# First weight chunk of the output tails stored 64 bytes into its tile, and the first product of each seven-product half 264 columns wide in place of two operand copies

## The chip, the cores and the metric

The kernel runs on one core of a Trainium2 chip. The metric is the device time of one execution in microseconds (us), the median of several runs. The kernel before took 1624.95 us, the median of three runs between 1624.73 and 1625.51.

## What is computed

A two-layer diffusion transformer on 256 image tokens and 256 context tokens of width 1024. Each layer is a half feed-forward, a mixer (attention in layer 0, an mLSTM in layer 1) and another half feed-forward, each behind a modulation by two conditioning vectors and followed by a layer norm. The part that matters here is the feed-forward, cut from the reference:

```python
def half_ffn(h, shift, scale, gate, w_in, w_out, g, b):
    xm = modulate(h, shift, scale)
    a, u = jnp.split(xm @ w_in, 2, axis=-1)
    y = (jax.nn.silu(a) * u) @ w_out
    return post_norm(h, 0.5 * gate * y, g, b)
```

Its hidden width is 2816, that is 22 blocks of 128. It runs four times: twice in layer 0 and once in layer 1 for both token groups (512 columns), and once more, at the very end, for the image tokens alone.

## The kernel before

**Operands.** Everything is float32 in storage. A product that must be exact to float32 is made of three products in `float32r`: each operand is split into a high and a low part, and `mm3` (L239) issues high times high, high times low and low times high into one PSUM tile. Activations lie transposed, 128 rows of features by tokens, so a product has a stationary weight block of 128 by 128 and a moving operand of 256 columns (one token group, `LAT` or `CTX`) or 512 (`BOTH`). The activations' two parts stand in `xh` and `xl` (L281), each feature block 512 columns and 64 more.

**Weights.** A chunk is 128 rows by 1024 columns, eight stationary blocks. SP loads it into a `raw` tile; `chunk` (L218) takes a tile of the ring `w` of seven (L215; 2112 columns of 4 bytes, which is 66 times 128 bytes), ACT casts the chunk into its first half as the high part (L225), and DVE subtracts to leave the low part in the second half (L230). An argument `sh` moves both parts `sh` columns into the tile; `SH` is 16 columns, 64 bytes. `Stream` (L143) fetches chunks in order and keeps the last; `Keep` (L158) keeps all of them, for weights that two passes use.

**A feed-forward** (`ffn`, L684) works in two halves of eleven hidden blocks. For each half it makes the eleven blocks of the hidden layer (the `in` part) and then the eight output blocks `d` (the `out` part), each the sum of 11 blocks, so 33 products of `mm3`. The output weights of a half are eleven chunks of eight blocks, numbered `d * 11 + i`: chunk 5 holds numbers 40 to 47. In the second half the first four output blocks are made for 512 columns at once with a `Stream` that moves nothing (`sh` 0). The last four (`TAIL`, L56) are made twice, for the image tokens and then for the context tokens, with 256 columns each, so that the norm of the image tokens starts while the context tokens are still in work. I call these the image tail and the context tail. Their weights come through a `Keep` with `SH` (L782) that takes over the chunk which the `Stream` holds at that moment, chunk 5: numbers 40 to 43 belong to the last block of the body, 44 to 47 to the tail, twelve products in each of the two tails. So chunk 5 stands at the start of its tile, and the six chunks behind it 64 bytes further. Between the products of the tails stand the statistics products of the norm (L447), issued at fixed places of a table (`TAILSTEP`, L99), some with 256 moving columns and some with one.

**The seven-product form.** In the second feed-forward of layer 0 and the first of layer 1, the second half makes its hidden blocks by `fast_in` (L626): seven block products of a Strassen kind instead of eight, each over four feature blocks, so 7 x 4 x 3 = 84 products of 256 columns for a hidden block and 924 for a half. The products are a11, a12, s1, s2, a22, s4 and s3, in that order, twelve instructions each. The sums of activations that they need are made before by `fast_sums` (L599) into the operand `made` during the out part of the first half. All weights here have `SH`. For the first hidden block of the half alone (`j == NFH`, L631), a22 does not read its operand from `made[2]`: two ACT copies (L635) put it into a tile of the ring `w`, `FLIP` = 56 columns in, which is 32 bytes past a step of 64 bytes.

**What sets the order.** TensorE takes its products in program order. ACT and DVE follow an order that a scheduler makes from priorities and dependencies; the ring of seven `w` tiles sets how far ahead weights are split.

Of the kernel before, what the change touches and what calls it, by code (L numbers as in the profile page):

```python
# [9 lines left out]
F32 = mybir.dt.float32  # L10
F32R = mybir.dt.float32r
# [7 lines left out]
P = 128  # L19
D = 1024  # L20
ND = D // P
T = 512
TL = 256
LAT = (0, 256)
# [3 lines left out]
NFH = 11  # L28
# [3 lines left out]
BLOCK = 64  # L32

SH = 16
# [9 lines left out]
WB = 7  # L44
# [11 lines left out]
TAIL = 4  # L56
# [31 lines left out]

SUMSAT = 4
FLIP = 56  # L90
BESIDE = {1: (), 2: (2, 3)}
PIECES = 4
DOTS = {
# [79 lines left out]
class Body:  # L173
# [23 lines left out]
    def mm(self):  # L197
        return self.t([P, 512], tag="mm", bufs=6, pool=self.pp)
# [37 lines left out]
            edge = mybir.DependencyInfo(mybir.DependencyClass.NoSync, mybir.DependencyReason.DATA)  # L236
            self.tc.add_manual_dep(ins.ins, last.ins.name, edge, reason="behind the start")

    def mm3(self, out, w, x, first, last, pin=False, group=True):  # L239
        (wh, wl), (xh, xl) = w, x  # L240
        mm = lambda *k, **kw: self.nc.tensor.matmul(*k, skip_group_check=not group, **kw)  # L241
        ins = mm(out, wh, xh, start=first, stop=False)
        if pin:
            self.pin(ins)
        mm(out, wh, xl, start=False, stop=False)
        mm(out, wl, xh, start=False, stop=last)

    def x(self, d, g):
        return self.xh[:, d, g[0] : g[1]], self.xl[:, d, g[0] : g[1]]
# [342 lines left out]
    def fast_operands(self, st):  # L592

        n = ND // 2 * TL
        x = self.t([P, 6 * n], F32R, pool=st)
        self.t([P, FLIP], pool=st)
        self.made = [[x[:, (2 * i + p) * n : (2 * i + p + 1) * n].rearrange("p (k f) -> p k f", f=TL) for p in range(2)] for i in range(3)]
# [28 lines left out]
    def fast_in(self, j, w_in, st):  # L626

        nc, V, S = self.nc, self.nc.vector, self.nc.scalar
        half = 4 * P
        t4 = self.made[2]  # L630
        if j == NFH:  # L631
            w = self.t([P, 2 * 1024 + BLOCK], F32R, tag="w", bufs=WB)
            t4 = [w[:, FLIP + i * 1024 : FLIP + (i + 1) * 1024].rearrange("p (k f) -> p k f", f=TL) for i in range(2)]
            for i in range(2):
                S.copy(t4[i], self.made[2][i].bitcast(F32))  # L635
        r0, r1 = (self.raw(w_in[2 * j + i]) for i in range(2))
        sums = self.t([P, 4 * half], tag="sums", bufs=1, pool=st)
        part = lambda x, i: x[:, i * half : (i + 1) * half]
        a11, a21, a12, a22 = part(r0, 0), part(r0, 1), part(r1, 0), part(r1, 1)
        s1, s2, s4, s3 = (part(sums, i) for i in range(4))  # L640
        add = lambda o, x, y: V.tensor_tensor(out=o, in0=x, in1=y, op=ALU.add)  # L641
        ws = [self.pair(sh=SH, n=half)] + [self.pair(sh=SH) for _ in range(3)]
        self.split(a11, *ws[0])
        self.split(r1, *ws[1])
        add(s1, a21, a22)
        add(s2, s1, a11)
        add(s4, s2, a12)
        add(s3, a11, a21)
        self.split(sums[:, : 2 * half], *ws[2])
        self.split(sums[:, 2 * half :], *ws[3])  # L650
        w = {n: [part(x, i) for x in ws[p]] for n, p, i in (
            ("a11", 0, 0), ("a12", 1, 0), ("a22", 1, 1), ("s1", 2, 0), ("s2", 2, 1), ("s4", 3, 0), ("s3", 3, 1),
        )}
        of = lambda k0, g: lambda k: self.x(k0 + k, g)
        made = lambda i: lambda k: [x[:, k, :] for x in self.made[i]]

        def product(o, name, x, first, last):
            for k in range(ND // 2):
                c = slice(k * P, (k + 1) * P)
                self.mm3(o, [y[:, c] for y in w[name]], x(k), first and k == 0, last and k == ND // 2 - 1, group=False)  # L660

        x, yv, z = self.mm()[:, :TL], self.mm(), self.mm()[:, :TL]
        y, v = yv[:, :TL], yv[:, TL:]
        a, u = self.tmp(), self.tmp()
        product(x, "a11", of(0, LAT), True, False)
        S.copy(a[:, :TL], x)
        product(y, "a12", of(ND // 2, LAT), True, True)
        product(v, "s1", of(0, CTX), True, False)
        S.copy(u[:, TL:], v)
        product(x, "s2", made(0), False, False)  # L670
        S.copy(a[:, TL:], x)
        product(z, "a22", lambda k: [x[:, k, :] for x in t4], True, True)
        S.copy(u[:, :TL], z)
        product(v, "s4", of(ND // 2, CTX), False, True)
        V.tensor_tensor(out=a, in0=a, in1=yv, op=ALU.add)
        S.activation(a, a, AF.Silu)
        product(x, "s3", made(1), False, True)
        u2 = u.rearrange("p (n f) -> p n f", n=2)
        V.scalar_tensor_tensor(u2, x[:, None, :].broadcast_to([P, 2, TL]), -1.0, u2, ALU.mult, ALU.subtract)
        V.tensor_tensor(out=a, in0=a, in1=u, op=ALU.mult)  # L680
        gh, gl = self.gt[j] = tuple(self.t([P, self.gw], F32R, tag=k, bufs=self.gn, pool=self.gp) for k in ("gh", "gl"))
        self.split(a, gh, gl)

    def ffn(self, layer, s, gate, groups, side, start=None, cpool=None):  # L684
# [4 lines left out]
        with self.tc.tile_pool(name=f"ffn{li}", bufs=1) as gp:  # L689
# [32 lines left out]
            w_in, w_out = self.a["ffn_in"][li], self.a["ffn_out"][li]  # L722
            stream = lambda j: Stream(self, [w_in[2 * j + i] for i in range(2)])
            for hf in range(2):
                js = list(range(hf * NFH, (hf + 1) * NFH))[0 if hf else done :]
                if hf == 0 and not start:
                    first = js[:LEAD]
# [6 lines left out]
                    j = first[-1]  # L734
                    ps = unit_in(j, ws[j], LAT, ks=k0)
                    assert not self.running
                    xs = {}
                    for k in BESIDE[li]:
                        xs[k] = [self.t([P, self.gw], F32R, tag=t, bufs=self.gn, pool=gp)[:, FLIP : FLIP + TL] for t in ("gh", "gl")]
                        for o, x in zip(xs[k], self.x(k, CTX)):  # L740
# [20 lines left out]
                    self.residual(2, self.pin)  # L761
                if not hf:
                    self.residual(len(self.later))
                w = Stream(self, [w_out[hf * NFH + i] for i in range(NFH)])
                body = ND - TAIL if hf else ND
                if fast:
                    more.close()
# [13 lines left out]
                if body < ND:  # L781
                    w = Keep(self, w.chunks, SH, w)  # L782
# [1000 lines left out]
```

## Time and profile before

| | us |
|---|---|
| median of 3 runs | 1624.95 |
| profiled execution, its own time | 1624.66 |
| its span in the trace | 1622.9 |
| TensorE matmul busy | 1608.2 |
| TensorE weight loads busy | 1450.3 |
| VectorE busy | 1349.3 |
| ScalarE busy | 749.0 |
| the four copies of L635, ScalarE | 1.05 each |

The profiled execution is 0.29 us below the median, and 1.76 us of it lie outside the span. A matmul's record goes on after the next one has begun (0.276 to 0.39 us long, with a next start every 0.113 to 0.227 us), so the busy share of TensorE says little, and the pace of its products is what to read: where a view in order of time joins n equal products into one piece, the pace is the piece's length less one record's length, divided by n - 1. The view in order of time gives, in each row, the start in us from the span's start, the length in us, the engine, the line, the operation with its tiles and shapes, and the count.

### The profile page before, as it was taken

What the parts mean: (1) busy time and instruction counts of PE and PEld (TensorE: products, weight loads), DVE (VectorE), ACT (ScalarE), POOL (GpSimd) and SP (SyncE); (2) the same over time, 40 slices, a digit from 0 to 9 for tenths busy, and PEclk for the clock granted to TensorE, in tenths of its full rate; (3) what the DMA queues carried; (4) which work ended last, traced back from release to release, by engine and by line L of the source; (5) the groups of instructions that cost most, each with busy time, mean ns of one, the idle gap of its engine ahead of it and who ended that gap; (6) DMA issues with size and microseconds to landing.
All of it is one profiled execution on the core that took longest, in us unless ns stands there. A gap on an engine that the chain in (4) does not pass through costs nothing. (4 is left out here: it accounts for less than half of the span.)

```text
span 1622.9 us, 26548 instructions
## 1 busy us (share of the span) xinstructions
PE 1608.2 (99%) x10280; PEld 1450.3 (89%) x10280; DVE 1349.3 (83%) x2687; ACT 749.0 (46%) x1276; POOL 62.4 (4%) x77
## 2 busy tenths in 40 slices
PE   9999999999999999999999999999999999999998
PEld 7888888889988998889999998889999989999986
DVE  7899978648879879999976979689967968897597
ACT  6522132314676443316652443336642657566542
POOL 0000000001011200000000100000001000020000
PEclk9999999999999999999999999999999999999999
DMA  9677765422203347633354258723372343437562
GB/s 358 220 250 238 237 207 184 141 66 85 66 2 99 136 144 228 212 104 118 117 175 151 79 180 289 245 64 106 109 238 83 98 130 92 151 98 259 170 181 91
DMA packets 72222, 251.56 MB, mean 155 GB/s; under 512 B 7960, under 2 KB 10776, under 8 KB 72096
## 3 DMA queue, kind: packets, MB, share of 16 engines
q1 hardware_dynamic: 71520, 249.09, 48.0%
q8 instruction: 80, 1.31, 0.3%
q10 hardware_dynamic: 576, 0.79, 0.1%
q14 instruction: 46, 0.38, 0.1%
HBM read 248.79 MB, written 1.05 MB: 154 GB/s over the span
## 5 line engine op out<-in xcount | busy, mean ns | idle before, releaser
L241 PE MATMUL t<-t,t 128*128 128x256 f32 (+2 forms) x8340 | 1307.7, 318 | 3.2 <-ACT t L225 1.1
L241 PEld LDWEIGHTS t<-t,t 128*128 128x128 f32 x8340 | 1175.8, 188 | 120.7 <-ACT t L225 2.0
L225 ACT CAST t<-t 128x1024 fp32r<-128x1024 f32 (+3 forms) x509 | 421.6, 850 | 479.3 <-PE t L241 225.0
L230 DVE TENSOR_TENSOR t<-t,t 128x256 fp32r<-128x256 f32 (+2 forms) x728 | 505.4, 729 | 110.7 <-ACT t L225 106.9
L350 DVE SCALAR_TENSOR_TENSOR t<-t,t 128x1024 bf16<-128x1024 f32 x224 | 260.7, 1220 | 0.0
L588 ACT ACTIVATE t<-t 128x512 f32<-128x512 f32 (+1 forms) x71 | 34.4, 489 | 98.8 <-PE t L241 97.8
L941 PE MATMUL t<-t,t 128*128 128x256 f32 (+1 forms) x256 | 79.3, 310 | 0.2 <-ACT t L541 0.2
L718 DVE SCALAR_TENSOR_TENSOR t<-t,t,t 128x256 f32<-128x256 f32 x96 | 42.7, 478 | 43.9 <-PE t L241 43.7
L943 PE MATMUL t<-t,t 128*128 128x256 f32 (+1 forms) x256 | 78.5, 307 | 0.1
L942 PE MATMUL t<-t,t 128*128 128x256 f32 (+1 forms) x256 | 78.3, 306 | 0.1
L589 DVE TENSOR_TENSOR t<-t,t 128x512 f32<-128x512 f32 (+1 forms) x71 | 39.0, 553 | 40.6 <-PE t L241 27.7
L484 POOL TENSOR_TENSOR t<-t,t 128x256 f32<-128x256 f32 x30 | 23.2, 774 | 1105.1 <-ACT t L474 1103.8
L869 PE MATMUL t<-t,t 128*128 128x512 f32 (+1 forms) x300 | 61.0, 364 | 0.4 <-DVE t L863 0.4
L869 PEld LDWEIGHTS t<-t,t 128*128 128x128 f32 x300 | 51.3, 189 | 10.0 <-DVE t L863 1.1
L474 ACT ACTIVATE t<-t 128x256 f32<-128x256 f32 x72 | 26.1, 412 | 65.8 <-DVE t L467 65.8
L1470 PE MATMUL t<-t,t 128*128 128x512 f32 (+2 forms) x276 | 55.7, 357 | 0.0
L1470 PEld LDWEIGHTS t<-t,t 128*128 128x128 f32 (+1 forms) x276 | 44.9, 183 | 11.0 <-issue 1.1
L942 PEld LDWEIGHTS t<-t,t 128*128 128x128 f32 x256 | 48.1, 188 | 3.3 <-DVE t L230 0.8
L941 PEld LDWEIGHTS t<-t,t 128*128 128x128 f32 x256 | 48.2, 188 | 3.2 <-ACT t L541 0.4
L943 PEld LDWEIGHTS t<-t,t 128*128 128x128 f32 x256 | 48.1, 188 | 2.8 <-DVE t L542 0.3
L541 ACT ACTIVATE t<-t,t 128x256 fp32r<-128x256 f32 x72 | 32.8, 502 | 31.1 <-DVE t L540 31.1
L641 DVE TENSOR_TENSOR t<-t,t 128x512 f32<-128x512 f32 x66 | 45.3, 687 | 0.4
(211 smaller groups left out, 1107.8 us busy)
## 6 DMA issues: line engine op xcount, KB each, us to landing
t<-in_ffn_in SPq DMA_DIRECT2D x168, 512.0 KB, 4.1
t<-in_ada_w SPq DMA_DIRECT2D x138, 512.0 KB, 4.4
t<-in_ffn_out SPq DMA_DIRECT2D x66, 512.0 KB, 4.4
t<-in_ffn_last SPq DMA_DIRECT2D x22, 512.0 KB, 3.5
t<-in_att_in SPq DMA_DIRECT2D x12, 512.0 KB, 3.5
t<-in_att_out SPq DMA_DIRECT2D x8, 512.0 KB, 3.6
t<-in_ml_qk SPq DMA_DIRECT2D x8, 512.0 KB, 3.7
t<-in_ml_v SPq DMA_DIRECT2D x8, 512.0 KB, 3.6
```

The source lines that it names most:

```text
L225: self.behind(self.nc.scalar.copy(h, x))
L230: self.behind(self.nc.vector.tensor_tensor(out=ls, in0=xs, in1=hs.bitcast(F32), op=ALU.subtract))
L241: mm = lambda *k, **kw: self.nc.tensor.matmul(*k, skip_group_check=not group, **kw)
L350: ins = nc.vector.scalar_tensor_tensor(self.tmp().bitcast(BF16), r, 1.0, self.cb[:, v, :], ALU.mult, ALU.mult, accum_out=to)
L589: V.tensor_tensor(out=sl, in0=sl, in1=pu[:, :n], op=ALU.mult)
L641: add = lambda o, x, y: V.tensor_tensor(out=o, in0=x, in1=y, op=ALU.add)
L718: V.scalar_tensor_tensor(z, y[:, gg[0] - t0 : gg[1] - t0], gate()[:, v, d : d + 1], z, ALU.mult, ALU.add)
L869: pin(nc.tensor.matmul(o, gs[g], ws[k][w][:, i : i + n], start=k == k0 and g == w == 0, stop=k == k1 - 1 and g == 1,))
L941: mm(o, self.xh[:, k, c], wh, start=k == 0, stop=False)
L942: mm(o, self.xh[:, k, c], wl, start=False, stop=False)
L943: mm(o, self.xl[:, k, c], wh, start=False, stop=k == ND - 1)
L1470: mm = lambda *k, **kw: pin(nc.tensor.matmul(*k, **kw))
```

## The change

Two things are changed. First, the stream of output weights of a feed-forward moves one chunk by `SH`, in the second half only: the one whose number is (8 - 4) * 11 // 8 = 5. This holds for the three feed-forwards that `ffn` makes. Second, in `fast_in` the two copies and their tile are gone, and a22 reads `made[2]` for every hidden block. The first product of a11 of the first hidden block (high part times high part of feature block 0) gets 264 columns instead of 256: it reads eight columns more of `xh`, and writes eight more of its PSUM tile. No instruction reads those eight.

```diff
+ODD = 8
...
-    def mm3(self, out, w, x, first, last, pin=False, group=True):
+    def mm3(self, out, w, x, first, last, pin=False, group=True, wide=()):
...
-        ins = mm(out, wh, xh, start=first, stop=False)
+        o, y = wide or (out, xh)
+        ins = mm(o, wh, y, start=first, stop=False)
...
-        t4 = self.made[2]
-        if j == NFH:
-            w = self.t([P, 2 * 1024 + BLOCK], F32R, tag="w", bufs=WB)
-            t4 = [w[:, FLIP + i * 1024 : FLIP + (i + 1) * 1024].rearrange("p (k f) -> p k f", f=TL) for i in range(2)]
-            for i in range(2):
-                S.copy(t4[i], self.made[2][i].bitcast(F32))
...
-        x, yv, z = self.mm()[:, :TL], self.mm(), self.mm()[:, :TL]
+        xx, yv, z = self.mm(), self.mm(), self.mm()[:, :TL]
+        x = xx[:, :TL]
...
-        product(x, "a11", of(0, LAT), True, False)
+        product(x, "a11", of(0, LAT), True, False, (xx[:, : TL + ODD], self.xh[:, 0, : TL + ODD]) if j == NFH else ())
...
-        product(z, "a22", lambda k: [x[:, k, :] for x in t4], True, True)
+        product(z, "a22", made(2), True, True)
...
-                w = Stream(self, [w_out[hf * NFH + i] for i in range(NFH)])
+                w = Stream(self, [w_out[hf * NFH + i] for i in range(NFH)], lambda c, hf=hf: SH if hf and c == (ND - TAIL) * NFH // ND else 0)
```

In the order of instructions a row names the tile that is written, then those that are read (the moving operand, then the weights). On TensorE, at the hand-over from the first half's output blocks to the first hidden block of the seven-product half in layer 0, the order before is this (t_67 and t_68 are `xh` and `xl`, t_7095 the weights of a11, t_7111 its PSUM tile):

```order
L241 MATMUL t_7046<-t_6623,t_7058 128x512
L241 MATMUL t_7046<-t_6624,t_7058 128x512
L241 MATMUL t_7046<-t_6623,t_7058 128x512
L241 MATMUL t_7111<-t_67,t_7095 128x256
L241 MATMUL t_7111<-t_68,t_7095 128x256
L241 MATMUL t_7111<-t_67,t_7095 128x256 x2
```

And now (t_7092 are the weights of a11, t_7108 its PSUM tile):

```order
L242 MATMUL t_7046<-t_6623,t_7058 128x512
L242 MATMUL t_7046<-t_6624,t_7058 128x512
L242 MATMUL t_7046<-t_6623,t_7058 128x512
L242 MATMUL t_7108<-t_67,t_7092 128x264
L242 MATMUL t_7108<-t_68,t_7092 128x256
L242 MATMUL t_7108<-t_67,t_7092 128x256 x2
```

Only the width of one product differs; every other instruction of TensorE stands where it stood, in this half and everywhere else. The shift of chunk 5 changes addresses alone and no row.

On ACT, ahead of the same half, the order before is this (t_6876 is `made`, t_67 the context columns of `xh`, t_7087 the tile of the two copies, t_7095 to t_7098 the weights of the first hidden block):

```order
L225 CAST t_67<-t_6985 128x2x256
L225 CAST t_6876<-t_6987 128x512
L225 CAST t_6876<-t_6985 128x512
L225 CAST t_6876<-t_7000 128x512
L635 CAST t_7087<-t_6876 128x1024
L225 CAST t_7095<-t_7090 128x512
L635 CAST t_7087<-t_6876 128x1024
L225 CAST t_7096<-t_7092 128x1024
L225 CAST t_7097<-t_7094 128x1024
L225 CAST t_7098<-t_7094 128x1024
```

And now (t_7092 to t_7095 are the weights of the first hidden block):

```order
L226 CAST t_7092<-t_7087 128x512
L226 CAST t_7093<-t_7089 128x1024
L226 CAST t_67<-t_6919 128x2x256
L226 CAST t_6876<-t_6921 128x512
L226 CAST t_6876<-t_6919 128x512
L226 CAST t_6876<-t_6934 128x512
L226 CAST t_67<-t_6985 128x2x256
L226 CAST t_6876<-t_6987 128x512
L226 CAST t_6876<-t_6985 128x512
L226 CAST t_6876<-t_7000 128x512
L226 CAST t_7094<-t_7091 128x1024
L226 CAST t_7095<-t_7091 128x1024
```

The two copies are gone, and the casts of the first two weight tiles stand ahead of those of the activation sums instead of behind them; the matching subtractions on DVE move the same way.

More of the change, by code (lines that the diff above doesn't have):

```diff
@@ L655, in fast_in, with product @@
         made = lambda i: lambda k: [x[:, k, :] for x in self.made[i]]
-        def product(o, name, x, first, last):
+        def product(o, name, x, first, last, wide=()):
             for k in range(ND // 2):
                 c = slice(k * P, (k + 1) * P)
-                self.mm3(o, [y[:, c] for y in w[name]], x(k), first and k == 0, last and k == ND // 2 - 1, group=False)
-        x, yv, z = self.mm()[:, :TL], self.mm(), self.mm()[:, :TL]
+                self.mm3(o, [y[:, c] for y in w[name]], x(k), first and k == 0, last and k == ND // 2 - 1, group=False, wide=() if k else wide)
+        xx, yv, z = self.mm(), self.mm(), self.mm()[:, :TL]
+        x = xx[:, :TL]
         y, v = yv[:, :TL], yv[:, TL:]
         a, u = self.tmp(), self.tmp()
-        product(x, "a11", of(0, LAT), True, False)
+        product(x, "a11", of(0, LAT), True, False, (xx[:, : TL + ODD], self.xh[:, 0, : TL + ODD]) if j == NFH else ())
         S.copy(a[:, :TL], x)
```

## The prediction

> **What bounds the kernel now.** I first read the page's busy times and slices, then the groups by line and shape, then the order of time on TensorE around the two places that change.
>
> ```profile
> span 1622.9 us, 26548 instructions
> PE 1608.2 (99%) x10280; PEld 1450.3 (89%) x10280; DVE 1349.3 (83%) x2687; ACT 749.0 (46%) x1276; POOL 62.4 (4%) x77
> PEclk9999999999999999999999999999999999999999
> ...
> L241 PE MATMUL t<-t,t 128*128 128x512 f32 x2892 | 662.3, 390 | 0.0
> L241 PE MATMUL t<-t,t 128*128 128x256 f32 x5304 | 629.8, 279 | 2.9 <-ACT t L225 1.1 <-DVE t L542 1.0 <-ACT t L541 0.5
> ```
>
> TensorE always has a product in work, at the full granted clock, and the 5304 products of 256 columns from `mm3` waited 2.9 us in all. Wherever this holds, only two things can change the time: the number of products and the pace at which one follows the other. So I read the pace, a piece's length less one record, over the gaps in it. The rows are start, length, engine, line, operation and count. These are the first seven-product half's start, its middle and the piece between, then the same three of the second half; ahead of them the 512-column products that come before.
>
> ```profile
> 725.64 11.72 PE L241 MATMUL t<-t,t 128*128 128x512 f32 x51
> 738.34 7.34 PE L241 MATMUL t<-t,t 128*128 128x256 f32 x61
> 743.64 1.57 PE L241 MATMUL t<-t,t 128*128 128x256 f32 x12
> 746.32 96.95 PE L241 MATMUL t<-t,t 128*128 128x256 f32 x854
> 1090.43 5.35 PE L241 MATMUL t<-t,t 128*128 128x256 f32 x44
> 1095.73 1.34 PE L241 MATMUL t<-t,t 128*128 128x256 f32 x10
> 1097.95 97.29 PE L241 MATMUL t<-t,t 128*128 128x256 f32 x857
> ```
>
> 512 columns: (11.72 - 0.39) / 50 = 0.2266 us. The half begins at (7.34 - 0.28) / 60 = 0.1177 us a product and from 746.3 goes on at (96.95 - 0.28) / 853 = 0.1133 us to its end. The second half does the same: 0.1178 at first, then 0.1133. The two stretches have equal shapes, the same placing of weights and, in these rows, the same clock:
>
> ```profile
> core 0: us, PE busy (x) PEld busy (x) DVE busy (x) ACT busy (x) POOL busy (x), PEclk, DMA share, GB/s
> 738.60:745.50 6.90, 6.90 (x61) 6.90 (x60) 5.25 (x9) 4.01 (x7) 0.00 (x0) 1.00 0.37 113
> 746.50:843.00 96.50, 96.50 (x854) 96.50 (x854) 90.35 (x119) 61.85 (x101) 0.00 (x0) 1.00 0.38 121
> ```
>
> So a row of such products has two lasting paces, which I call the 118 pace and the 113 pace. What stands between them in both halves is the piece of twelve at 743.64 (and at 1095.73), the a22 product that reads the copies of L635, 32 bytes off a 64-byte step. It runs at (1.57 - 0.28) / 11 = 0.117 itself, and four products behind it the 113 pace is there.
>
> The tails show a third pace. Rows: the twelve products of chunk 5 in the image tails of the first two feed-forwards, each followed by the same tail's other products, and those twelve in the third.
>
> ```profile
> 348.34 1.12 PE L241 MATMUL t<-t,t 128*128 128x256 f32 x8
> 349.42 11.71 PE L241 MATMUL t<-t,t 128*128 128x256 f32 x98
> 873.29 1.24 PE L241 MATMUL t<-t,t 128*128 128x256 f32 x9
> 874.37 11.71 PE L241 MATMUL t<-t,t 128*128 128x256 f32 x98
> 1225.26 1.24 PE L241 MATMUL t<-t,t 128*128 128x256 f32 x9
> ```
>
> With weights at the start of their tile the pace is (1.12 - 0.28) / 7 = 0.120 and twice (1.24 - 0.28) / 8 = 0.120; with weights 64 bytes further it is (11.71 - 0.28) / 97 = 0.1178, the 118 pace. In the context tails, of the first feed-forward (two rows), the second (four) and the third (two):
>
> ```profile
> 362.00 2.17 PE L241 MATMUL t<-t,t 128*128 128x256 f32 x17
> 364.24 1.36 PE L241 MATMUL t<-t,t 128*128 128x256 f32 x10
> 887.17 1.98 PE L241 MATMUL t<-t,t 128*128 128x256 f32 x16
> 889.22 1.24 PE L241 MATMUL t<-t,t 128*128 128x256 f32 x9
> 890.54 0.87 PE L241 MATMUL t<-t,t 128*128 128x256 f32 x6
> 898.87 11.31 PE L241 MATMUL t<-t,t 128*128 128x256 f32 x93
> 1239.02 1.98 PE L241 MATMUL t<-t,t 128*128 128x256 f32 x16
> 1241.06 1.36 PE L241 MATMUL t<-t,t 128*128 128x256 f32 x10
> ```
>
> Ahead of chunk 5 the first is at the 118 pace, (2.17 - 0.28) / 16 = 0.118; the second and third are at the 113 pace, (1.98 - 0.28) / 15 = 0.1135. Chunk 5's twelve run at 0.120 (364.24, 889.22, 1241.06), and what follows them (890.54) is at (0.87 - 0.28) / 5 = 0.118: the twelve products have thrown the row out of the 113 pace.
>
> **The seven-product halves: the copies.** Two copies a half are removed, on ACT:
>
> ```profile
> L635 ACT CAST t<-t x4: 1047/1049/1056, 730.5 to 1081.7; 128x1024 fp32r<-128x1024 f32 x4
> ...
> who waited for it (us, times):
> ```
>
> That is 4 x 1.05 = 4.2 us of ACT, for which nobody waited; the first starts at 730.5, 7.8 us ahead of the row at 738.34, the last 8.7 ahead of that at 1090.43. I cost their removal at nothing. What hides them is the last 512-column products before the half (51 in the row of 725.64), and ACT is 46% busy. The ring of `w` tiles is used once less a half, so ACT and DVE split the first weights earlier and the activation sums later. Those sums are first needed by s2, 36 products or 4.2 us into the half, so I put no wait there.
>
> What the copies did for TensorE is the question. Without them a22 reads operands on a 64-byte step and, by the rows above, would leave the 118 pace alone. The wide first product must do their work.
>
> **The wide product itself.** Eight columns of 256 at the 113 pace are 8 x 0.1133 / 256 = 0.0035 us, 0.007 for both halves; as a whole further step of sixteen columns at most twice that.
>
> **What the wide product does to the pace.** No product in the trace is 264 columns wide, and none stands alone between 512 and 256 columns. The nearest rows are in the mLSTM's projections, where groups with products of 258 columns (L1340 and L1342, two columns past a step of 64 bytes) are followed directly by `mm3` products of 256 columns and 64-byte-shifted weights. There are seven such hand-overs; these are the rows of 256 behind each:
>
> ```profile
> 1356.20 2.20 PE L241 MATMUL t<-t,t 128*128 128x256 f32 x18
> 1361.78 2.20 PE L241 MATMUL t<-t,t 128*128 128x256 f32 x18
> 1369.40 2.40 PE L241 MATMUL t<-t,t 128*128 128x256 f32 x19
> 1375.33 2.32 PE L241 MATMUL t<-t,t 128*128 128x256 f32 x19
> 1383.22 2.20 PE L241 MATMUL t<-t,t 128*128 128x256 f32 x18
> 1388.85 4.70 PE L241 MATMUL t<-t,t 128*128 128x256 f32 x40
> 1397.27 3.56 PE L241 MATMUL t<-t,t 128*128 128x256 f32 x30
> ```
>
> Six give (2.20 - 0.28) / 17 = 0.113 or the like; the third gives (2.40 - 0.28) / 18 = 0.118. The copies were two of two. So a step of columns that is not whole sixteens ends in the 113 pace eight times in nine, and 512 columns followed straight by 256 at the 118 pace (738.34, 1090.43). I take it that the wide product brings the 113 pace, some five products behind it, and that it then lasts, as it does for 97 us. Gain a half: 64 products now at the 118 pace (48 ahead of a22, its twelve, four behind) less five, 59 x (0.1177 - 0.1133) = 0.26, less 0.004; both halves **-0.51 us**. The bounds: -0.28 a half at best; at worst the 118 pace for the 860 products behind the present change of pace, 860 x 0.0044 = +3.8 a half.
>
> The Trainium skill bears on this ("TensorE: Matmul & The Clock Gate", "Back-to-back issue gap"): it gives the warm gap of an isolated product by its columns alone, N / 2.4 + 2.5 ns, 109.2 for 256. By that the change would be the eight columns, 3.3 ns a half, and nothing else. The trace disagrees: 113.3, 117.7 and 120 ns for the same N at the same clock.
>
> **Chunk 5.** Twelve products in each of six tails go from 0.120 to the pace around them. In the image tail 512-column products come straight ahead, which in both halves above gave the 118 pace; then 12 x (0.120 - 0.1178) = 0.026 us, three times. The same in the first context tail. In the other two the 113 pace stands ahead and, without the twelve, should go on through them and the nine behind, up to the single-column statistics products: 12 x (0.120 - 0.1135) + 9 x (0.118 - 0.1135) = 0.078 + 0.041 = 0.12 us each. There it ends, by a like place in attention's tail: 0.114 ahead of those products ((0.96 - 0.28) / 6), 0.118 behind ((0.99 - 0.28) / 6).
>
> ```profile
> 541.65 0.96 PE L241 MATMUL t<-t,t 128*128 128x256 f32 x7
> ...
> 543.13 0.99 PE L241 MATMUL t<-t,t 128*128 128x256 f32 x7
> 374.44 7.42 PE L241 MATMUL t<-t,t 128*128 128x256 f32 x64
> ```
>
> Sum: 4 x 0.026 + 2 x 0.12 = **-0.34 us**. The twelve 512-column products of chunk 5 in each body (36 in all) get shifted weights, which no 512-column product of `mm3` has now. A weight load takes 0.19 us and their gap is 0.227, so I put nothing; an upper bound from the step between 0.1133 and 0.120, doubled for twice the columns, is 36 x 0.013 = +0.5, and the same below nothing is excluded, since 0.2266 is the pace of all rows seen. What I can't price is luck behind the statistics products: at one and the same place of the context tail the first feed-forward goes on at (7.42 - 0.28) / 63 = 0.1134 (374.44) and the second at (11.31 - 0.28 - 0.19) / 92 = 0.118 (898.87; 0.19 is a first gap of 0.306 less 0.118). Such a stretch is worth 93 x 0.0044 = 0.41 us either way, and the change moves the tails by tenths of a microsecond. I allow one or two stretches, 0.6 us.
>
> **The sum.** 1624.66 for the profiled execution less 0.51 less 0.34 is 1623.8. That execution lay 0.29 below the median, so the median should be 1624.95 - 0.85 = **1624.1**. Own range with luck and the 512-column bound: 1623.3 to 1625.2.
>
> **Rivals.**
>
> *The wide product doesn't change the pace (slower).* A single longer product may leave the two streams, moving operand and weights, where they were as soon as the next one begins; for this speaks the third of the seven rows, and that one product is far less than the twelve misplaced ones or a group with many of 258. Then both halves stay at the 118 pace to their end, since in them nothing else ever changed it: +3.8 each, less the tails' 0.34. 1624.95 + 7.6 - 0.3 = 1632.2. If one half only, 1628.2. It decides with the first ten products of each half. Against it: eight of nine. Chance 0.15 for both, 0.03 for one.
>
> *The image tails start at the 113 pace (faster).* The 512-column products ahead of them now have shifted weights too, which the halves' entries had not. Then the 97 products behind the burst gain 97 x 0.0044 = 0.43 and the twelve 0.05 more, three times: 1624.1 - 1.4 = 1622.7. Chance 0.13.
>
> *Placement isn't the cause.* The skill says in the same page ("Step-by-step: what each phase is for") that loading the next weights "doesn't steal SBUF read bandwidth from the running matmul". As a mechanism here: weight loads and moving reads don't meet, both paces come from elsewhere, say from what ACT and DVE do meanwhile, and neither shift nor width matters. The switch at 745.6 and 1097.6 would come anyhow and the tails stay: 1624.95. Against it: in both halves the switch follows the misplaced product within four products, at 7.5 us into each, and 0.120 goes with chunk 5 alone in all six tails. Chance 0.07.
>
> **How the numbers follow.** My forecast has 0.62. With the faster tails and the unchanged case it is 0.82, so the range goes from 1622.7 less 0.7 for luck, 1622.0, to 1625.4, over the unchanged case and the forecast's upper end; the slower rival's 0.18 is left out. About 0.2% (3.25 us) is what a measurement of this kernel can tell from no change. Faster than that needs the fast tails and every stretch of luck: 0.02. Slower is the first rival in both halves, and about a third of its single case: 0.16. Within: 0.82.
>
> **What would show it.** In the changed kernel the piece from the half's sixth product to its end is one row at 0.1133 us, about 919 products, in both halves; six bursts of 0.120 are gone; the context tails of the second and third feed-forward hold 0.1135 until the single-column products; ACT has four casts less and no new wait of TensorE stands at either half's start. A half that runs at 0.1177 beyond its first ten products would prove the forecast wrong; a tail stretch at another pace would move the size by 0.4 each.

## The result, and the profile after

| | before | after |
|---|---|---|
| median | 1624.84 us (6 runs, 1624.2 to 1625.72) | 1632.2 us (6 runs, 1630.51 to 1632.91) |
| span of the profiled execution | 1622.9 us | 1630.3 us |
| ratio of the times | | 1.0044 (1.0031 to 1.0057) |

The kernel became slower by 7.4 us. The first rows to read are the page's, with the groups of `mm3` by shape behind them.

```profile
span 1630.3 us, 26554 instructions
PE 1615.5 (99%) x10280; PEld 1458.2 (89%) x10280; DVE 1351.5 (83%) x2687; ACT 746.3 (46%) x1272; POOL 62.6 (4%) x77
PEclk9999999999999999999999999999999999999999
```

```profile
L242 PE MATMUL t<-t,t 128*128 128x512 f32 x2892 | 662.5, 390 | 0.0
L242 PE MATMUL t<-t,t 128*128 128x256 f32 x5302 | 637.2, 281 | 3.6 <-ACT t L543 1.1 <-DVE t L544 1.0 <-ACT t L226 1.0
```

The busy time is what the group covers of the span, records that overlap counted once. Products of 512 columns: 662.3 before, 662.5 now. Products of 256: 629.8 before, 637.2 now. Those 7.4 us are as much as the whole difference; the waits ahead of the group grew by 0.7 us, the clock is full in every slice, and the busy times of VectorE, ScalarE and GpSimd moved by at most 2.7 us. So it is more time per product, not more waiting. The order of time on TensorE says where. These are the start and the middle of the first seven-product half, then of the second.

```profile
737.19 8.06 PE L242 MATMUL t<-t,t 128*128 128x264 f32 x67
746.03 97.21 PE L242 MATMUL t<-t,t 128*128 128x256 f32 x824
1094.22 2.05 PE L242 MATMUL t<-t,t 128*128 128x256 f32 x16
1098.11 96.15 PE L242 MATMUL t<-t,t 128*128 128x256 f32 x815
```

The first half begins at (8.06 - 0.28) / 66 = 0.118 and stays there: (97.21 - 0.28) / 823 = 0.1178. Before, the window from 746.3 to 843 us held 856 products; now it holds 824. The second half does the same, (2.05 - 0.28) / 15 = 0.118 and (96.15 - 0.28) / 814 = 0.1178. The 113 pace never comes in either half. Between the first products of the two halves, in the two traces:

| stretch | before, us | after, us | difference |
|---|---|---|---|
| start to the first half | 738.11 | 737.19 | -0.92 |
| first half, its 924 products | 105.00 | 108.83 | +3.83 |
| between the halves | 246.97 | 247.84 | +0.87 |
| second half, its 924 products | 105.00 | 108.84 | +3.84 |
| from there to the end | 427.82 | 427.60 | -0.22 |

The two halves are +7.67 of the span's +7.4. Of the other terms, -0.75 lies ahead of the 300th product of the kernel, where nothing was changed, and most of the +0.87 is one stretch that the change doesn't touch either. First the row of after, then that of before:

```profile
938.05 18.18 PE L242 MATMUL t<-t,t 128*128 128x256 f32 x153
```

```profile
936.83 17.86 PE L241 MATMUL t<-t,t 128*128 128x256 f32 x154
```

The first runs at (18.18 - 0.28) / 152 = 0.1178 throughout; the second covers one more product in less time, since most of it is at the 113 pace. This is the luck for which the prediction allowed 0.6: in the traces of the ten kernels that this document compares by their times (the benches left out), which all leave this stretch alone, it runs at 113 in five and at 118 in five.

The tails of the changed kernel. The rows are the last output blocks of the body of the first feed-forward (512 columns, ahead of chunk 5, then chunk 5 itself), the image tails of the first and second, and pieces of the context tails at chunk 5 of the first, second and third.

```profile
336.70 7.64 PE L242 MATMUL t<-t,t 128*128 128x512 f32 x33
344.64 2.73 PE L242 MATMUL t<-t,t 128*128 128x512 f32 x11
347.44 12.77 PE L242 MATMUL t<-t,t 128*128 128x256 f32 x107
876.28 12.76 PE L242 MATMUL t<-t,t 128*128 128x256 f32 x107
363.24 1.98 PE L242 MATMUL t<-t,t 128*128 128x256 f32 x16
890.74 1.46 PE L242 MATMUL t<-t,t 128*128 128x256 f32 x11
1248.84 1.81 PE L242 MATMUL t<-t,t 128*128 128x256 f32 x14
```

The image tails are at (12.77 - 0.28) / 106 = 0.1178 from their first product, the third too (105 products in 12.53 us from 1232.72): the bursts of 0.120 are gone. The context tails stand at 0.1133 in the first feed-forward, (1.98 - 0.28) / 15, and at 0.118 in the second and third, (1.46 - 0.28) / 10 and (1.81 - 0.28) / 13. And the 512-column products of chunk 5 have become slower: (2.73 - 0.39) / 10 = 0.234 against (7.64 - 0.39) / 32 = 0.2266 ahead of them.

### The profile page after: what moved, and what is told of

It reads as the page before. It is cut to its first block, busy times and chain, and to the rows that moved or that the text cites. A ratio compares the mean times of both kernels' runs of the same rounds, so it can differ in the third digit from the quotient of the medians.

```text
span 1630.3 us, 26554 instructions
## 1 busy us (share of the span) xinstructions
PE 1615.5 (99%) x10280; PEld 1458.2 (89%) x10280; DVE 1351.5 (83%) x2687; ACT 746.3 (46%) x1272; POOL 62.6 (4%) x77
```

## The experiments

My theory after the result: the pace of a long row of 256-column products depends on where their operands lie and on what the row has met last; the two misplaced copies had brought the 113 pace, and the 264-column product brings nothing. Against it stand three others. The shift of chunk 5 could have changed the entry of the halves. The wide product could itself hold the row at the 118 pace, so that a half left alone would switch. Or the switch could belong to something that went with the copies on ACT and DVE and not to any operand of TensorE.

**One part at a time.** Three kernels. The kernel before with the shift of chunk 5 alone:

```diff
-                w = Stream(self, [w_out[hf * NFH + i] for i in range(NFH)])
+                w = Stream(self, [w_out[hf * NFH + i] for i in range(NFH)], lambda c, hf=hf: SH if hf and c == (ND - TAIL) * NFH // ND else 0)
```

> The kernel before with chunk 5 moved 64 bytes, and with its copies and products of 256 columns left as they were. Theory (the wide product fails to bring the 113 pace): both seven-product halves change to 0.113 us a product behind the a22 of the first hidden block, so the time is that of the kernel before within 0.7 us. Rival (the moved chunk is at fault, by way of the buffers or the tails): some 1632 us, as the changed kernel.

The changed kernel without the shift:

```diff
-                w = Stream(self, [w_out[hf * NFH + i] for i in range(NFH)], lambda c, hf=hf: SH if hf and c == (ND - TAIL) * NFH // ND else 0)
+                w = Stream(self, [w_out[hf * NFH + i] for i in range(NFH)])
```

> The kernel before with the copies dropped and the first product 264 columns wide, chunk 5 unmoved. Theory: both halves stay at 0.118 us a product to their ends, 2 x 860 products x 0.0044 us = 7.6 us slower than before, 1632 to 1633. Rival (the moved chunk is at fault): as before, 1625.

The changed kernel with 256 columns in the first product too, so without copies and without a wide product:

```diff
-        product(x, "a11", of(0, LAT), True, False, (xx[:, : TL + ODD], self.xh[:, 0, : TL + ODD]) if j == NFH else ())
+        product(x, "a11", of(0, LAT), True, False)
```

> The changed kernel with the first product 256 columns wide again; the copies stay dropped. If the wide product does nothing at all: the same as the changed kernel, 1632 within 0.7 us, and 0.118 in both halves. If it does something that is lost later (a pace that changes for a while, or a cost), the two differ in the first products of the halves; if the eight columns alone keep the pace slow, this one is at 1624.

| | median, us | ratio to before |
|---|---|---|
| shift alone | 1625.35 (10 runs) | 1.0002 (0.9992 to 1.0011) |
| wide product alone | 1633.06 (4 runs) | 1.0049 (1.0033 to 1.0066) |
| shift, no copies, no wide product | 1633.49 (4 runs) | 1.0051 (1.0036 to 1.0066) |

The middles of both halves, first with the shift alone:

```profile
746.11 97.11 PE L241 MATMUL t<-t,t 128*128 128x256 f32 x855
1098.08 96.12 PE L241 MATMUL t<-t,t 128*128 128x256 f32 x846
```

With the wide product alone:

```profile
746.12 97.09 PE L242 MATMUL t<-t,t 128*128 128x256 f32 x823
1098.05 96.15 PE L242 MATMUL t<-t,t 128*128 128x256 f32 x815
```

And with neither copies nor a wide product:

```profile
746.03 97.21 PE L242 MATMUL t<-t,t 128*128 128x256 f32 x824
1098.03 96.15 PE L242 MATMUL t<-t,t 128*128 128x256 f32 x815
```

Read the counts: 855 and 846 where the copies are, 823 or 824 and 815 where they are not. The last two kernels and the changed one have the same pace to a thousandth of a microsecond. So the whole loss comes with the copies' removal, the 264-column product changes nothing that lasts, and the shift of chunk 5 costs or brings nothing that this comparison can tell from zero.

**Does any wide product bring the 113 pace?** A bench inside the changed kernel: ahead of each hidden block of the halves but the first, three products of 512 columns into an unused tile are to bring back the state of the entry, and then a11's products get a width or a start of their own from a table.

```diff
+        for _ in range(3 if (self.lab - 1) % NFH else 0):
+            nc.tensor.matmul(dummy, w["a11"][0][:, :P], self.xh[:, 0, :T], start=True, stop=True, skip_group_check=True)
+        wider, off, at = LAB.get(self.lab - 1, (0, 0, ()))
...
+                n, o = (wider, off) if 3 * k + p in at else (0, 0)
```

> A bench inside the changed kernel: ahead of each hidden block of the two seven-product halves but the first of each stand three more 512-column products into an unused PSUM tile, which should bring the 118 pace back (control: hidden block 1 of the first half, with nothing else), and then the twelve products of a11 are varied: wider by 8, 2, 16 or 4 columns, or starting 8, 4 or 16 columns into the operand, for one, two, three, six or all twelve. The blocks with another start read other columns, so their numbers are not the reference's. Read: the pace of the 72 products behind a11. Theory A (one product is too little; several in a row that don't end on a whole sixteen columns change it): 113 behind twelve of 264 or 258, 118 behind one; likewise by start. Theory B (only the start counts, width never): 118 behind every width, 113 behind twelve that start 8 columns in. Theory C (a single wide product works, but not directly behind 512 columns): 118 behind one at the first place, 113 behind one at the fourth.

It took 1644.8 us, and what it shows first is a fault of the bench. Two blocks were left alone, the second of the first half and the last of the second; these are the products behind a11 in each.

```profile
750.64 8.32 PE L250 MATMUL t<-t,t 128*128 128x256 f32 x72
...
1205.75 5.93 PE L250 MATMUL t<-t,t 128*128 128x256 f32 x49
```

(8.32 - 0.28) / 71 = 0.1132 and (5.93 - 0.28) / 48 = 0.1177. Two blocks with nothing changed gave the two paces, so three products do not bring back one state, and single outcomes behind them prove little. One block of this bench has no dummies ahead of it, the first of the second half, and there a11's first product keeps its 256 columns but starts eight columns further into its operand. These are the products behind a11:

```profile
1101.67 8.32 PE L250 MATMUL t<-t,t 128*128 128x256 f32 x72
```

That is the 113 pace, (8.32 - 0.28) / 71, straight behind 512-column products. The kernel with neither copies nor a wide product stays at 118 at this place. So another start can do it without any further column, as far as one run shows. I made the dummies nine, and put single widths and starts into the table:

```diff
-        for _ in range(3 if (self.lab - 1) % NFH else 0):
+        for _ in range(9 if (self.lab - 1) % NFH else 0):
```

> The bench again with nine 512-column products ahead of each hidden block (three left an unsettled pace of 231 to 236 ns and, with nothing else, once the 113 and once the 118 pace), and one product varied: the first, wider by 2, 4, 6, 8, 10, 12, 14, 16, 24 or 32 columns, or starting 2, 4, 8, 12 or 16 columns into the operand; further the first two or three wider by 8, the fourth by 16, and 16 and 2 more columns at the two natural entries, where no added product stands ahead. Blocks with another start read other columns, so their numbers are not the reference's. Theory D (one product is enough, but its size decides, and 8 columns is a bad one): both blocks without a change at 118, 8 at 118, and several other widths, 2 and 16 among them, at 113, with equal outcomes at the natural entries. Theory A (several products are needed): all single ones at 118. Theory E (the outcome hangs on what went before, not on the width): the two blocks without a change differ, or the natural entries differ from the added ones.

1671.49 us. The rows: nine dummies, the 72 products behind a11 in the block that was left alone, then twice the twelve of a11 (the row shows the width of its first product) and the 72 behind them, with eight columns more and with sixteen, and at last the other block left alone.

```profile
748.35 2.25 PE L673 MATMUL t<-t,t 128*128 128x512 f32 x9
...
751.86 8.64 PE L250 MATMUL t<-t,t 128*128 128x256 f32 x72
...
797.68 1.58 PE L678 MATMUL t<-t,t 128*128 128x264 f32 x12
799.10 8.64 PE L250 MATMUL t<-t,t 128*128 128x256 f32 x72
...
845.67 1.56 PE L678 MATMUL t<-t,t 128*128 128x272 f32 x12
847.07 8.32 PE L250 MATMUL t<-t,t 128*128 128x256 f32 x72
...
1234.49 5.72 PE L250 MATMUL t<-t,t 128*128 128x256 f32 x49
```

Left alone, the early block ran at (8.64 - 0.28) / 71 = 0.1177 and the late one at (5.72 - 0.28) / 48 = 0.1133. In both benches such a block came out at the other pace than the block ahead of it: twice from 118 to 113, twice from 113 to 118. So the dummies did not wipe out what stood ahead of them. A likely reason shows in their own pace: they read the weights of a11, which are shifted by 64 bytes, and run at (2.25 - 0.39) / 8 = 0.2325, in turns of 231 and 236 ns, where the 512-column products ahead of a half run at 226.7. It is the same slower row that chunk 5 now has. In this bench a11's operand 16 columns wider gave the 113 pace and eight wider the 118 pace; eight wider in the first two products gave 113, in the first three 118, and sixteen wider in the fourth 118; starts 2 and 4 columns further gave 118, 8, 12 and 16 further 113. With such an entry this is no proof. But at the first block of each half, which has no dummies, 16 columns more (first half) and 2 more (second half) both gave 113, 72 products in 8.32 us. That is a lead: in the kernel the first product of a half can be given other widths.

**Sixteen and two columns in the kernel itself.** The changed kernel with one number changed:

```diff
-ODD = 8
+ODD = 16
```

> The changed kernel with the first product 272 columns wide instead of 264 (16 more, not 8). Theory D (one product suffices, its size decides): at the natural entry of the first half 16 more gave the 113 pace in the bench, so both halves run at 0.113 from some six products on: 7.6 us faster than the changed kernel, 1624.5, the same as before within 0.7 us. Theory E (the outcome hangs on what went before): one or both halves stay at 0.118, 1628 or 1632.

And `ODD = 2`:

> The changed kernel with the first product 258 columns wide (2 more). Theory D: 2 more gave the 113 pace at the natural entry of the second half in the bench, so 1624.5 as with 16. Theory E: one or both halves at 0.118, 1628 or 1632.

Sixteen took 1625.04 us (11 runs; ratio 1.0000, 0.9991 to 1.0009), two took 1624.49 (11 runs; 0.9994, 0.9986 to 1.0003). The halves with sixteen, in rows that begin at the tenth product of the first half and the sixth of the second:

```profile
740.03 102.16 PE L242 MATMUL t<-t,t 128*128 128x256 f32 x900
1091.82 102.39 PE L242 MATMUL t<-t,t 128*128 128x256 f32 x902
```

and with two, beginning within the first twenty products:

```profile
739.95 100.24 PE L242 MATMUL t<-t,t 128*128 128x256 f32 x883
1091.78 98.42 PE L242 MATMUL t<-t,t 128*128 128x256 f32 x867
```

(102.16 - 0.28) / 899 = 0.1133, (100.24 - 0.28) / 882 = 0.1133, and the same in the second halves. This settles the main question from the other side: there are no copies here, ACT and DVE have the same instructions as in the changed kernel, and one product out of 924 that is wider by 16 or by 2 columns moves the whole half. A half now takes 104.75 us from its first product to the next 512-column one, against 105.00 before and 108.83 in the changed kernel. The pace hangs on TensorE's own products, and at this place the number of columns of one decides it. A sixteen is a whole step of 64 bytes, so my "step of columns that is not whole sixteens" is not what counts.

**A clean bench.** The bench again, with dummies that read weights at the start of a 128-byte step (from `xh`), in the first half; in the second half no dummies, so that each block enters at the pace that the block ahead of it left.

```diff
+        for _ in range(9 if 0 < self.lab - 1 < NFH else 0):
+            nc.tensor.matmul(dummy, self.xh[:, 7, :P], self.xh[:, 0, :T], start=True, stop=True, skip_group_check=True)
```

> The bench with a better reset in the first half: the nine added 512-column products take their weights from a place that is a multiple of 128 bytes, so that they should settle at 226.7 ns like the natural ones (with weights 64 bytes further they ran at 231 to 236 in turn, and two blocks without a change differed). First half: nothing, then the first product wider by 2, 4, 6, 8, 10, 12, 14, 16, 24. Theory D: nothing 118, 2 and 16 at 113, 8 at 118, as at the natural entries. Theory E: differences between equal widths remain. Second half: no reset at all; the first block 2 wider, which should bring the 113 pace, then the first product of each following block wider by 2, 16, 4, 6, 24, 8, 2, 12, 16. If the 113 pace is where any disturbance ends, it stays; if a width only moves from one pace to the other by its size, some of these bring the 118 pace back.

1650.8 us. The dummies' last three products are 225 to 227 ns apart each time. Rows as above, of the first half: nothing, two columns more, eight, sixteen.

```profile
750.48 1.58 PE L678 MATMUL t<-t,t 128*128 128x256 f32 x12
751.89 8.64 PE L250 MATMUL t<-t,t 128*128 128x256 f32 x72
...
762.44 1.54 PE L678 MATMUL t<-t,t 128*128 128x258 f32 x12
763.82 8.32 PE L250 MATMUL t<-t,t 128*128 128x256 f32 x72
...
797.24 1.58 PE L678 MATMUL t<-t,t 128*128 128x264 f32 x12
798.66 8.64 PE L250 MATMUL t<-t,t 128*128 128x256 f32 x72
...
844.76 1.56 PE L678 MATMUL t<-t,t 128*128 128x272 f32 x12
846.16 8.32 PE L250 MATMUL t<-t,t 128*128 128x256 f32 x72
```

Every row of 72 has one of two lengths: 8.32 us, the 113 pace, or 8.64 to 8.65, the 118 pace. Behind 512-column products:

| columns more in a11's first product | 0 (twice) | 2 | 4 | 6 | 8 | 10 | 12 | 14 | 16 | 24 |
|---|---|---|---|---|---|---|---|---|---|---|
| ns a product behind it | 118 | 113 | 113 | 113 | 118 | 113 | 118 | 118 | 113 | 113 |

Most cells rest on one block of one run; behind the unsettled dummies of the bench before, 2 and 10 had given 118. The kernels agree with this table where they overlap: 0 and 8 stay at 118, 2 and 16 go to 113. The second half, where there are no dummies: its second and third block, and the seventh.

```profile
1123.27 1.57 PE L678 MATMUL t<-t,t 128*128 128x258 f32 x12
1124.68 8.64 PE L250 MATMUL t<-t,t 128*128 128x256 f32 x72
1133.16 1.55 PE L678 MATMUL t<-t,t 128*128 128x272 f32 x12
1134.54 8.32 PE L250 MATMUL t<-t,t 128*128 128x256 f32 x72
...
1172.04 1.56 PE L678 MATMUL t<-t,t 128*128 128x264 f32 x12
1173.44 8.32 PE L250 MATMUL t<-t,t 128*128 128x256 f32 x72
```

Two columns more, entered from the 113 pace, threw the row to 118; sixteen from there brought it back; and eight columns more, entered from 118, gave 113. In all, from the 113 pace: 2 (both times), 4 and 24 ended at 118, 16 stayed at 113, and a block left alone stayed. From the 118 pace: 6, 8, 12 and 16 ended at 113. Hence eight columns are not idle in themselves; they seem idle at that place, straight behind 512-column products.

**Eight columns, three products later.** If so, the kernel's own eight columns should work on a11's fourth product, which has three 256-column products at the 118 pace ahead of it.

```diff
-                self.mm3(o, [y[:, c] for y in w[name]], x(k), first and k == 0, last and k == ND // 2 - 1, group=False, wide=() if k else wide)
+                self.mm3(o, [y[:, c] for y in w[name]], x(k), first and k == 0, last and k == ND // 2 - 1, group=False, wide=wide if k == 1 else ())
...
-        product(x, "a11", of(0, LAT), True, False, (xx[:, : TL + ODD], self.xh[:, 0, : TL + ODD]) if j == NFH else ())
+        product(x, "a11", of(0, LAT), True, False, (xx[:, : TL + ODD], self.xh[:, 1, : TL + ODD]) if j == NFH else ())
```

> The changed kernel with the same 264 columns on the fourth product of a11 instead of the first, so not directly behind the 512-column products but inside the stretch at the 118 pace. In the bench 8 more columns brought the 113 pace there (second half, no reset), and the 118 pace directly behind 512 columns. Theory F (the outcome depends on the pace it meets and on the size together): both halves go to 0.113 from the eighth product or so, 1624.5, 7.6 us faster than the changed kernel. Rival (8 columns is a bad size anywhere): both stay at 0.118, 1632.

1624.72 us (10 runs; ratio 1.0002, 0.9992 to 1.0011). The two halves:

```profile
738.76 101.48 PE L242 MATMUL t<-t,t 128*128 128x256 f32 x894
1090.74 99.44 PE L242 MATMUL t<-t,t 128*128 128x256 f32 x876
```

(101.48 - 0.28) / 893 = 0.1133. A product with the same number of columns, three places later, is worth 1632.2 - 1624.7 = 7.5 us.

**More places.** If one product can set the pace, the tails could be set too. Sixteen columns in the halves, and in the first product of each of the four output blocks of an image tail:

```diff
+                    more_ = (y[:, : TL + ODD], gh[:, : TL + ODD]) if g == LAT and i == 0 else ()
-                    self.mm3(y[:, : t1 - t0], w(d * NFH + i), (gh[:, t0:t1], gl[:, t0:t1]), i == 0, i == NFH - 1)
+                    self.mm3(y[:, : t1 - t0], w(d * NFH + i), (gh[:, t0:t1], gl[:, t0:t1]), i == 0, i == NFH - 1, wide=more_)
```

> The changed kernel with 16 more columns instead of 8 (as e4_odd16), and the first product of each of the four output blocks of the three image tails 16 wider too. If 16 more columns bring the 113 pace from the 118 pace here as in the bench, and keep it when they meet it, the 97 products up to the first statistics products and the 23 behind them run at 0.113: 3 x 120 x 0.0044 = 1.6 us less than e4_odd16, minus some 0.03 us for each of the twelve wide products, so about 1623.8 with e4's 1625.0, and some 1.4 us below the kernel before. Rival: behind products with moved weights, which run at 231 to 236 ns in turn, or from block to block, the pace goes back and forth, and half of it is lost.

1623.71 us (11 runs; 0.9994, 0.9985 to 1.0003). Rows: the first image tail, and a stretch of `mm3` that the edit leaves alone.

```profile
348.82 11.37 PE L242 MATMUL t<-t,t 128*128 128x256 f32 x98
...
1458.79 26.43 PE L242 MATMUL t<-t,t 128*128 128x256 f32 x223
```

The same stretch in the kernel before:

```profile
1458.95 26.23 PE L241 MATMUL t<-t,t 128*128 128x256 f32 x230
```

The tail gains: (11.37 - 0.28) / 97 = 0.1143, three disturbances by the later wide products included, where before had 11.71 us for as many. But the stretch runs at (26.43 - 0.28) / 222 = 0.1178, where before had (26.23 - 0.28) / 229 = 0.1133. What three such tails gain, 3 x (11.71 - 11.37) = 1.0 us, this one stretch, 223 x (0.1178 - 0.1133) = 1.0 us, takes back. So I tried to set the pace at nineteen places: once in each image tail, in two blocks of each context tail, and in the four opening image blocks of two feed-forwards. The lines that choose them:

```diff
+                lead = g == LAT and ps is None
...
+                        wide = (o[:, : n + ODD], self.xh[:, 0, : n + ODD]) if lead and k == 0 and not part else ()
...
+                    if not i and g == LAT and d == body:
+                        wide = bank[:, ODD : 2 * ODD + TL], gh[:, : TL + ODD]
+                    if not i and g == CTX and d in (body + 1, body + 2):
+                        wide = bank[:, : TL + ODD], gh[:, TL - ODD :]
```

> e4_odd16 with the 16 more columns at 17 further places where the 118 pace was seen or likely: the first product of each image tail (not of its later blocks, where e7_tails16 paid some 0.03 us each for a pace that was already 113), the first product of the second and third block of each context tail (these read 16 columns to the left, so they start 64 bytes off), and the first product of the four image blocks that open the next feed-forward in two places. If each brings the 113 pace up to the next statistics products: 1.3 us in the image tails, up to 1.1 in the context tails and up to 1.0 in the opening blocks, so some 1622.5, 2 to 2.5 us below the kernel before. Rival: where the pace happens to be 113 the same product costs 0.03 us or throws it to 118, and a start 64 bytes off acts differently; then no better than e7_tails16, 1623.7, or worse.

1624.02 us (11 runs; 0.9995, 0.9985 to 1.0005). One opening block, with its wide product in the row:

```profile
900.09 6.64 PE L242 MATMUL t<-t,t 128*128 128x256 f32 x55
...
907.63 4.41 PE L242 MATMUL t<-t,t 128*128 128x272 f32 x36
```

Ahead of it (6.64 - 0.28) / 54 = 0.1178, and behind it (4.41 - 0.28) / 35 = 0.118: sixteen columns, which worked in both halves, did nothing here. In the tails they were followed by the 113 pace at seven of nine places. Where they missed, they stood inside a row at the 118 pace, as the fourth product of the second bench did; but from such a row they had also worked, in the clean bench. So the columns and the pace that they meet don't fix the outcome alone. No version beat the kernel before by more than its interval.

## Why the prediction was wrong

**The step that failed** is the one under "What the wide product does to the pace": "I take it that the wide product brings the 113 pace". From six of seven hand-overs behind 258-column groups and two behind misplaced copies I made a rule, a step of columns that is not whole sixteens ends in the 113 pace, and applied it to one product of 264 columns straight behind 512-column ones, a case that no row held. Eight columns do nothing there, sixteen (whole) do it, and two do it at that place and undo it from the 113 pace. Nine observations of two other disturbances were a frequency for those, not for this. The kernel with 256 columns in that product takes 108.83 us a half, as the one with 264 does. The forecast of -0.51 us became +7.67. The price of the pace itself was right: with 16 or 2 columns, or with eight on the fourth product, a half took 104.74 to 104.77 us against 105.00 before, the 0.26 forecast for a wide product that works.

**The rival that came true** is "The wide product doesn't change the pace": its time, 1632.2, is the median measured, and its term of 3.8 a half is the measured 3.83 and 3.84. Its price was sound because it came from the kernel's own rows (860 products, two lasting paces) and needed no idea of the cause. That it meets the median to the tenth is luck: it holds the -0.34 of the tails, which did not come, and untouched stretches moved by up to 0.9 us. What was wrong is the chance, 0.15. Its stated reason, that a single product is too little, fell: with 2 or 16 columns a single one is enough.

**Placement isn't the cause** fell too, in what it said of the halves and of chunk 5. Without copies the halves never switched by themselves, and with the work of ACT and DVE unchanged one wider product switched them. What switched them there was a width; that the place of an operand changes a pace is shown for chunk 5's weights and, in one block of the first bench, for a start. The Trainium skill's sentence that loading the next weights "doesn't steal SBUF read bandwidth from the running matmul" ("TensorE: Matmul & The Clock Gate", "Step-by-step: what each phase is for") would, read as a rule for the pace, give no room for a pace that the placing of weights changes. In this kernel the pace went from 0.120 to 0.1178 for chunk 5 in the image tails, and from 0.2266 to 0.234 in its 512-column products.

**The image tails at the 113 pace** did not come: 0.1178 from the first product. Shifted weights in the 512-column products ahead of them made those slower and left the entry as it was.

**Chunk 5.** The bursts of 0.120 went, as predicted. Two terms were mis-sized. The 36 products of 512 columns, put at nothing with +0.5 as a bound, cost 36 x (0.234 - 0.2266) = +0.27. And the context tails of the second and third feed-forward were not at the 113 pace ahead of chunk 5 but at 118, so the 0.12 each had nothing to keep; in the first, predicted at 118, the pace was 113. From chunk 5's first 512-column product to the first single-column statistics product, the three feed-forwards together took 63.87 us before, 64.14 with the shift alone and 63.98 in the changed kernel, where -0.34 was predicted. The median of the shift alone, at 1.0002, doesn't decide it: its interval, -1.3 to +1.8 us, would hold -0.34 as well.

**Two readings.** The prediction says that the sums made late are first needed by s2, 36 products into the half. In the kernel s1, 24 products in, already reads the context columns of `xh` that the same step rewrites; no wait of TensorE came of it. And (0.96 - 0.28) / 6 is 0.113, not 0.114, on which nothing hangs.

**What held**: as time on ACT, the copies' 4.2 us cost and saved nothing; no new wait of TensorE stands at the halves; the eight columns themselves are too small to see (108.83 us a half with and without them); and the luck of untouched stretches stayed within some 0.9 us.

**Open**: why 8, 12 and 14 columns more keep the 118 pace behind 512-column products while 2, 4, 6, 10, 16 and 24 end it, and why the answer is another behind another entry. The runs show which, not why. Nor was it taken apart what in the copies had brought the 113 pace: their place 32 bytes off, their tile, or something else that went with them.

## What to carry to other kernels

Where a row of equal products shows two lasting paces, whatever stands just ahead of it may be holding the faster one, however useless it looks: before it is removed, the price of its absence is the slower pace over the whole row, and that price needs no theory. A remedy seen to work with other sizes or at other places is no evidence for this size at this place; here it would have taken one row behind a 264-column product. And a single product of another width is a cheap lever, to be tried at several widths on the chip, at the place itself.

## What the runs showed of the hardware

- At the full granted clock, products of 256 columns with a weight load each ran at 0.1133, 0.1178 or 0.120 us, and products of 512 columns at 0.2266 or about 0.233. For chunk 5, weights 64 bytes into their tile removed the 0.120 at 256 columns and brought 0.234 at 512.
- The pace is a state that lasts: 0.1133 (with 16 columns more in the first product) or 0.1178 (without) over 900 products in a row that are the same in both kernels.
- One product with 2 columns more than its 923 neighbours changed the state for 100 us, about 4 us a half (108.83 to 104.74). Which way it goes depends on its columns and on what it meets: in the settled cases two more led to 113 from behind 512-column products, and both times to 118 from the 113 pace. These two alone don't fix it: sixteen more from inside the 118 pace led to 113 in one block of a bench and left the 118 pace in an opening block.
